# Attention values and denominators in one full-width matmul over [V|ones|V], shifted V and odd bias tables copied by DMA, and newly searched priorities

## The chip, the cores and the metric

The kernel runs as one program on the 8 cores of one Trainium2 chip. Cores 0 to 3 are one die, 4 to 7 the other. Cores 0 and 4 hold the beginning of a sequence and run one of two programs in the kernel ("first"); the other six run the second ("rest"). The metric is the time in microseconds (us) on the device of the slowest core. Some executions fall into a slower state, in which the cores of one die show a lower granted TensorE clock and the time is some per cent longer; only executions in the fast state are compared here. PE, DVE, ACT, POOL and SP are the engines (TensorE, VectorE, ScalarE, GpSimd, SyncE); on this kernel POOL issues the transfers of weights and SP those of outputs and small things.

## The reference

Four residual layers over one stream of 2 x 8192 tokens of width 1024, with 16 meta tokens put in front. Layers 0 and 3 mix by attention, layer 1 by a short gated convolution, layer 2 by pooling; a SwiGLU network follows each. The change touches the attention only:

```python
# 16 heads, 4 KV heads, head width 64, window 128, block 128
qkv = h @ w_qkv + b_qkv
...
s_band = einsum('bnqkgd,bnskd->bnkgqs', qb, k_band) + bias_band      # 2 blocks of keys
s_meta = einsum('bnqkgd,bmkd->bnkgqm', qb, km) + bias_meta           # 16 meta keys
p = softmax(concatenate([s_meta, s_band, sink_b], axis=-1))
o_r = einsum('bnkgqm,bmkd->bnqkgd', p_meta, vm) + einsum('bnkgqs,bnskd->bnqkgd', p_band, v_band)
return concatenate([o_m, o_r], axis=1) @ w_o + b_o
```

## The kernel before

The tokens of a core are worked in three groups, so there are 12 steps of a mixer and a network (layer 0 to 3 times group 0 to 2). The host program builds a list of operations with their dependences, and a list scheduler, steered by tables of priorities found by a search, puts them into one fixed order for each engine.

One unit of attention takes 64 queries of 4 heads for two KV heads: scores (PE, two row-tiled matmuls side by side), exponential (ACT), multiplication with a table of exponentials of the bias (DVE, into sb_P), values and denominators (PE), logarithm and exponential for the reciprocal of the denominator (ACT), product (DVE).

```python
# values: two KV heads side by side, 64 columns of the array each; then ones for the denominator
def av(e):
    for c, vf in ((0, va), (1, vb)):
        for kv in range(2):
            e.matmul(psum[kv*64:(kv+1)*64, O, 0:W], lhsT=vf(2*p+kv), rhs=P[...], start=(c==0), stop=(c==1))
    for c in range(2):
        for kv in range(2):
            ins = e.matmul(psum[kv*64:(kv+1)*64, O, 256:256+W], lhsT=one1, rhs=P[...], start=(c==0), stop=(c==1))
g.op("pe",  ..., av, R=[Pv, ...] + vk, W=[O], tag="av")
g.op("act", ..., R[:, 0:W] = Ln(bank(O)[:, 256:256+W]),  tag="den")
g.op("act", ..., R[:, 0:W] = Exp(-R[:, 0:W]),            tag="rden")
g.op("dve", ..., Q[:, ...] = bank(O)[:, 0:W] * R[:, 0:W], tag="omul")
...
# V of a block is kept three times: sb_Vt, and shifted with the meta tokens' V in sb_Vu and sb_Vw
g.op("act", ..., VU[0:64, sl, :] = VT_[0:64, sl, :],   tag="vu")
g.op("act", ..., VW[64:nr, sl, :] = VT_[64:nr, sl, :], tag="vw")
...
# the score of a unit lists the keys of V (vk) among what it reads, so it waits for V as well
g.op("pe", ..., sc, R=qk + kk + vk, W=[S], tag="score")
```

den and omul of one unit are one instruction each, of all 128 partitions: KV head 0 lies in partitions 0 to 63 and KV head 1 in 64 to 127 at the same columns.

The softmax here doesn't subtract the row's maximum and nothing guards it: scores larger than these inputs give would overflow.

## Time and profile before

| | before |
|---|---|
| time, median of 5 executions | 2690.76 us (2686.96 to 3039.39) |
| spans of the cores in the profiled execution | 2661.1 to 2669.8 us, clock 0.996 to 0.998 |
| PE, DVE, ACT busy on the slowest core (2) | 2628.2, 1565.4, 1331.8 us |
| PE idle on that core (span less busy) | 41.6 us |

The page of the profile gives, for the slowest core, busy time with its share of the span, and the chain of waits that ended last:

```profile
span 2669.8 us, 51871 instructions; the slowest of 8 cores (2661.1 to 2669.8 us)
...
PE 2628.2 (98%) x18296; PEld 1673.7 (63%) x18296; DVE 1565.4 (59%) x3259; ACT 1331.8 (50%) x2651; POOL 500.9 (19%) x951
...
PE 93%; DMA 2%; ACT 2%; issue 1%; DVE 1%; POOL 0%; POOLq 0%; DVEq 0%; ACTq 0%
...
```

The table of stretches gives the busy time of each engine in a stretch (start and end in us, length; then PE, weight loads, DVE, ACT, POOL, each with its count of instructions; clock, DMA share, GB/s):

```profile
...
core 2: us, PE busy (x) PEld busy (x) DVE busy (x) ACT busy (x) POOL busy (x), PEclk, DMA share, GB/s
0.00:140.00 140.00, 121.47 (x1033) 79.75 (x1034) 88.71 (x161) 97.47 (x189) 22.61 (x46) 0.95 0.58 126
140.00:440.00 300.00, 293.80 (x2253) 183.17 (x2252) 194.43 (x360) 194.43 (x399) 53.93 (x102) 1.00 0.67 106
440.00:1840.00 1400.00, 1396.17 (x9054) 880.20 (x9052) 822.43 (x1854) 603.56 (x1172) 275.92 (x522) 1.00 0.70 108
1840.00:2440.00 600.00, 597.24 (x4550) 395.59 (x4549) 349.19 (x670) 343.19 (x712) 114.67 (x217) 1.00 0.73 112
...
```

Of PE's 41.6 us of idle, 18.5 lie before 140 us, and 12.8 between 140 and 2440 us, although layers 0 and 3 with their attention lie in 20 to 440 and about 1700 to 2440 us. PE hardly ever waits, so only less work on PE, or an earlier start, can help. That is what the waits of PE on this core say too (what was waited for: us in all, times, longest):

```profile
...
PE ps L1464 <- DVE sb_P L1474: 6.8, 7, 3.6
PE ps L1216 <- ACT sb_sq L1210: 3.7, 3, 2.5
...
PE ps L1499 <- DVE sb_P L1474: 1.1, 1, 1.1
...
```

The groups of the instructions that the change splits (count after the x, busy us, then mean ns of one; then idle time before them), the product on DVE of core 2 first:

```profile
...
L1512 DVE TENSOR_TENSOR sb_qo<-ps,sb_R 128x256 bf16<-128x256 f32 x108 | 43.4, 416 | 10.0 <-ACT sb_R L1511 9.6 <-issue 0.3
...
```

and on ACT, the exponential (L1511) and the logarithm (L1510):

```profile
...
L1511 ACT ACTIVATE sb_R<-sb_R 128x256 f32<-128x256 f32 x128 | 51.0, 417 | 1.7 <-ACT sb_R L1510 0.4
L1510 ACT ACTIVATE sb_R<-ps 128x256 f32<-128x256 f32 x128 | 47.7, 381 | 57.5 <-PE ps L1505 54.0 <-DVE sb_h L1299 2.3 <-DVE sb_g L1852 0.2
...
```

### The profile page before, as it was taken

To read this page: it belongs to the slowest core of one execution; us is meant where nothing else is said; L and a number is where in the kernel's file an instruction comes from. 1 tells how busy PE (TensorE), PEld (TensorE's weight loads), DVE (VectorE), ACT (ScalarE), POOL (GpSimd) and SP (SyncE) were. 2 spreads that over 40 slices of the span, in tenths; PEclk is the share of its full clock that TensorE was granted. 3 is DMA by queue.
4 is the path that set the end of the run, shared out by engine and by line. 5 is a ranking of instruction groups with operands and counts; after the bars stand their busy time and mean duration, and the time that the engine had idled before them with its cause. 6 is when DMAs were issued, how large, how long until landed. Compare 5 with 4: busy or idle time off the path is not lost.

```text
span 2669.8 us, 51871 instructions; the slowest of 8 cores (2661.1 to 2669.8 us)
## 1 busy us (share of the span) xinstructions
PE 2628.2 (98%) x18296; PEld 1673.7 (63%) x18296; DVE 1565.4 (59%) x3259; ACT 1331.8 (50%) x2651; POOL 500.9 (19%) x951
## 2 busy tenths in 40 slices
PE   8999999999999999999999999999999999999998
PEld 5556665666666666655666666566566777656665
DVE  5785467455455555675685667446554665665534
ACT  6794566344243424353545534464553854744533
POOL 2021121211122212211111222112112221111110
PEclk9999999999999999999999999999999999999999
DMA  7476675766677767767657787658658878857873
GB/s 161 99 109 106 102 111 88 115 104 102 102 113 107 111 107 109 116 101 106 103 88 110 115 125 120 108 87 135 101 76 130 115 108 133 130 90 104 151 108 85
DMA packets 143446, 293.07 MB, mean 110 GB/s; under 512 B 15968, under 2 KB 22256, under 8 KB 142928
## 3 DMA queue, kind: packets, MB, share of 16 engines
q0 software_dynamic: 135840, 280.19, 67.6%
q1 hardware_dynamic: 7344, 9.47, 1.3%
q8 instruction: 154, 2.52, 0.4%
q14 instruction: 108, 0.88, 0.1%
HBM read 550.27 MB, written 8.28 MB: 209 GB/s over the span
## 4 chain that ended last, share of the span: by engine, by line
PE 93%; DMA 2%; ACT 2%; issue 1%; DVE 1%; POOL 0%; POOLq 0%; DVEq 0%; ACTq 0%
PE ps L1288 88%; PE ps L1499 1%; PE ps L1464 1%; PE ps L1505 1%; PE ps L1403 1%; PE ps L1806 1%; DMA sb_h<-x 0%; DMA sb_P<-xh 0%; DVE sb_P L1474 0%; DMA sb_ring<-ffn_gu 0%; DMA sb_ring<-attn_o 0%; DMA sb_ring<-attn_q 0%; PE ps L1228 0%; ACT sb_sq L1210 0%; ACT sb_ms L1139 0%
## 5 line engine op out<-in xcount | busy, mean ns | idle before, releaser
L1288 PE MATMUL ps<-sb_aF,sb_ring 128*128 128x384 bf16 (+4 forms) x8576 | 1342.5, 314 | 5.9 <-DVE sb_g L1852 1.6
L1288 PEld LDWEIGHTS ps<-sb_aF,sb_ring 128*128 128x128 bf16 x8576 | 826.3, 98 | 481.5 <-issue 39.0
L1288 PE MATMUL ps<-sb_g,sb_ring 128*128 128x384 bf16 (+4 forms) x4400 | 680.6, 315 | 2.9 <-DVE sb_g L1255 1.8
L1288 PEld LDWEIGHTS ps<-sb_g,sb_ring 128*128 128x128 bf16 x4400 | 427.8, 98 | 242.0 <-issue 11.8
L1848 DVE TENSOR_TENSOR sb_t<-sb_t,ps 128x384 f32<-128x384 f32 (+4 forms) x528 | 275.8, 523 | 431.5 <-ACT sb_t L1846 424.3
L1842 ACT ACTIVATE sb_t<-ps 128x384 f32<-128x384 f32 (+4 forms) x528 | 243.3, 461 | 497.0 <-PE ps L1288 494.5
L959 POOL DMA_DIRECT2D sb_ring<-ffn_gu x528 | 279.6, 534 | 1015.0 <-PE ps L1288 929.1
L1210 ACT ACTIVATE sb_sq<-sb_h 128x768 bf16<-128x768 f32 (+4 forms) x216 | 170.6, 796 | 427.2 <-DVE sb_h L1299 261.5
L1299 DVE TENSOR_TENSOR sb_h<-ps,sb_h 128x384 f32<-128x384 f32 (+4 forms) x432 | 226.8, 525 | 204.7 <-PE ps L1288 203.7
L1852 DVE TENSOR_TENSOR sb_g<-sb_t,ps 128x384 bf16<-128x384 f32 (+4 forms) x528 | 274.5, 522 | 108.7 <-PE ps L1288 100.6
L1844 ACT ACTIVATE sb_t<-sb_t,sb_ones 128x384 f32<-128x384 f32 (+4 forms) x528 | 310.3, 589 | 30.2 <-ACT sb_t L1842 0.7
L1288 PE MATMUL ps<-sb_aM,sb_ring 128*128 128x384 bf16 (+4 forms) x1952 | 322.6, 317 | 1.7 <-DMA sb_ring<-attn_q 0.9
L1846 ACT ACTIVATE sb_t<-sb_t 128x384 f32<-128x384 f32 (+4 forms) x528 | 261.8, 497 | 28.4 <-ACT sb_t L1844 0.7
L1288 PEld LDWEIGHTS ps<-sb_aM,sb_ring 128*128 128x128 bf16 x1952 | 189.9, 98 | 109.7 <-issue 7.7
L959 POOL DMA_DIRECT2D sb_ring<-ffn_dn x192 | 101.7, 532 | 592.5 <-PE ps L1288 519.3
L1474 DVE TENSOR_TENSOR sb_P<-ps,sb_ms 128x1024 bf16<-128x1024 f32 x128 | 154.7, 1220 | 64.2 <-ACT ps L1469 63.9
L1288 PE MATMUL ps<-sb_qo,sb_ring 128*128 128x384 bf16 (+3 forms) x1024 | 163.3, 315 | 1.4 <-DMA sb_ring<-attn_o 1.4
L1469 ACT ACTIVATE ps<-ps 128x1024 f32<-128x1024 f32 (+2 forms) x134 | 130.4, 990 | 10.6 <-PE ps L1464 10.1
L1288 PEld LDWEIGHTS ps<-sb_qo,sb_ring 128*128 128x128 bf16 x1024 | 99.8, 98 | 55.8 <-issue 2.8
L1301 DVE SCALAR_TENSOR_TENSOR sb_h<-ps,sb_cst,sb_h 128x384 f32<-128x384 f32 (+4 forms) x144 | 82.4, 583 | 65.7 <-PE ps L1288 51.8
L1223 DVE TENSOR_TENSOR sb_sq<-sb_sq 128x768 bf16<-128x768 bf16 (+4 forms) x156 | 81.7, 526 | 47.9 <-ACT sb_sq L1210 46.7
L1255 DVE SCALAR_TENSOR_TENSOR sb_aF<-sb_h,sb_cst,sb_rs 128x384 bf16<-128x384 f32 (+4 forms) x192 | 103.8, 581 | 3.6 <-ACT sb_rs L1233 2.9
(119 smaller groups left out, 1384.3 us busy)
## 6 DMA issues: line engine op xcount, KB each, us to landing
sb_ring<-ffn_gu POOLq DMA_DIRECT2D x528, 256.0 KB, 6.2
sb_ring<-ffn_dn POOLq DMA_DIRECT2D x192, 352.0 KB, 5.9
sb_ring<-conv_in POOLq DMA_DIRECT2D x72, 256.0 KB, 5.7
sb_ring<-attn_o POOLq DMA_DIRECT2D x48, 256.0 KB, 9.9
sb_ring<-attn_q POOLq DMA_DIRECT2D x40, 256.0 KB, 7.0
sb_ring<-conv_out POOLq DMA_DIRECT2D x24, 256.0 KB, 6.8
sb_ring<-attn_k POOLq DMA_DIRECT2D x11, 512.0 KB, 7.4
sb_ring<-attn_v POOLq DMA_DIRECT2D x11, 512.0 KB, 12.9
```

The source lines that it names most:

```text
L959: e.dma_start(out=ring[:, o.off:o.off + o.n], in_=o.src).then_inc(sem(o.dop[0]), 16)
L1210: lambda e, sv=sv, c=c: e.activation(out=ap(sv)[:, 0:2 * n].rearrange("p (a b) -> p a b", a=2), in_=src(2 * c, 2 * c + 2), func=AF.Square),
L1255: lambda e, k=k: e.scalar_tensor_tensor(out=dst[:, k, c0 - goff:c1 - goff], in0=h1(k, c0, c1), scalar=gam[:, gi * KC + k:gi * KC + k + 1], ...
L1288: i = e.matmul(bank(pv)[:, 0:n], lhsT=wap(u, woff + k * wst, M), rhs=rhs(k), start=(k == 0), stop=(k == nk - 1))
L1299: f = lambda e: e.tensor_tensor(out=h1(m, c0, c1), in0=bank(pv)[:, 0:n], in1=h1(m, c0, c1), op=ALU.add)
L1469: g.op("act", act_ns(4 * W), lambda e: e.activation(out=sp3(), in_=sp3(), func=AF.Exp, scale=0.125), R=[S], W=[S], tag="exp")
L1474: g.op("dve", dve_ns(4 * W), lambda e: e.tensor_tensor(out=pp(), in0=sp3(), in1=ebt, op=ALU.mult), R=[S, ("eb", p, odd)], W=[Pv], tag="ebm ...
L1842: g.op("act", act_ns(n), lambda e, pg=pg, tv=tv, n=n: e.activation(out=ap(tv)[:, 0:n], in_=bank(pg)[:, 0:n], func=AF.Exp, scale=-1.0), R=[ ...
L1844: g.op("act", act_ns(n, True, True), lambda e, tv=tv, n=n: e.activation(out=ap(tv)[:, 0:n], in_=ap(tv)[:, 0:n], func=AF.Ln, bias=ones1[:], ...
L1846: g.op("act", act_ns(n, True), lambda e, tv=tv, n=n: e.activation(out=ap(tv)[:, 0:n], in_=ap(tv)[:, 0:n], func=AF.Exp, scale=-1.0), R=[tv] ...
L1848: g.op("dve", dve_ns(n), lambda e, pg=pg, tv=tv, n=n: e.tensor_tensor(out=ap(tv)[:, 0:n], in0=ap(tv)[:, 0:n], in1=bank(pg)[:, 0:n], op=ALU ...
L1852: g.op("dve", dve_ns(n), lambda e, pu=pu, tv=tv, n=n, fj=fj, a=a, b=b: e.tensor_tensor(out=gg[:, fj, a - goff:b - goff], in0=ap(tv)[:, 0:n ...
```

## The change

The intent: PE is the limit, and every change between row-tiled scores, column-tiled values and full-width projections costs PE a gap. If values and denominators come from one full-width matmul, they need no mode of their own. A stored block of V becomes [V0|ones|V1] for each pair of KV heads, 192 columns. Columns 0 to 127 give V0 over its denominators, columns 64 to 191 the denominators over V1. ACT, which den now burdens more, is relieved of the V copies and of the copies that make the odd bias tables; these become transfers issued by SP. The tables of priorities were searched anew. Only the attention of the first group of layer 0 stays tiled.

```diff
-MODES = {"score": 1, "scorem": 1, "av": 2, "avm": 2, "vmeta": 2}
+MODES = {"score": 1, "scorem": 1, "av": 2, "avm": 2}
+TILED_AV = ((0, 0),)
+VB = 384
-RING = 16400
+RING = 15744
...                                                   # PLACES: all priorities and places of loads are new
-                    g.op("act", ..., act(lambda o_=o_: o_, lambda i_=i_: i_, AF.Copy), ..., tag="ebodd")
+                    g.op("sp", ..., lambda e, o_=o_, i_=i_: e.dma_start(out=o_, in_=i_), ..., dma="odd%d" % nload[0], tag="ebodd")
...
-            g.op("act", act_ns(256, True), lambda e: e.copy(out=VU[0:64, sl, :], in_=VT_[0:64, sl, :]), ..., tag="vu")
-            g.op("act", act_ns(256, True), lambda e: e.copy(out=VW[64:nr, sl, :], in_=VT_[64:nr, sl, :]), ..., tag="vw")
+            v_copy(VU, slice(0, 64), sl, "Vu")       # e.dma_start on SP
+            if 2 * t + 3 <= lay.blocks[5][-1]:
+                v_copy(VW, slice(64, nr), sl, "Vw")
...                                                   # V of the meta tokens projected once, not twice
+                def av(e):
+                    for kv in range(2):
+                        for c in cs:
+                            o_ = p * 192 + kv * 64
+                            ins = e.matmul(bank(O)[:, 256 * kv:256 * kv + W], lhsT=vs[c][:, o_:o_ + 128], rhs=pr(kv, c), start=(c == cs[0]), stop=(c == cs[-1]))
+                g.op("pe", 2 * len(cs) * pe_ns(W), av, R=[Pv] + vk, W=[O], tag="avf" + m_)
+                for kv in range(2):
+                    g.op("act", act_ns(W), ... ap(R)[kv*64:(kv+1)*64, 0:W] = Ln(bank(O)[64-kv*64:128-kv*64, 256*kv:256*kv+W]), tag="den")
...
+            for rows, o_ in ((slice(0, 128), 0),) if tiled else ((slice(0, 64), 0), (slice(64, 128), 256)):
+                g.op("dve", dve_ns(W), ... Q[rows, ...] = bank(O)[rows, o_:o_+W] * ap(R)[rows, 0:W], tag="omul")
```

The two KV heads now stand at different columns of the bank, so den and omul become two instructions of 64 partitions each.

## The prediction

> **What bounds it now.** TensorE. The page of the slowest core (core 2, one of six with the "rest" program) gives a span of 2669.8 us, PE busy 98%, DVE 59%, ACT 50%; the chain of waits is 93% PE. The table of stretches leaves PE idle about 24 us up to 140 us, 13 us in the next 2500 us, 10 us in the last 30 us. After the start only less PE time can help.
>
> **What the change does to PE.** Streaming time stays. In PE's timeline two 64-column value matmuls of width 256 run at once, a pair every 0.11 us, so a unit of 8 takes 0.44 us; four full 128-column matmuls of width 256 also start every 0.11 us. What goes is the change of array mode. The Trainium skill, "TensorEngine Tiling (Array Packing)", Key Properties, says that changing the tiling mode drains the engine. The trace agrees: the last pair before a full matmul takes 0.21 us instead of 0.11; 8 full 384-wide matmuls take 1.40 us instead of 1.31 when a tiled group follows. A switch costs 0.10 to 0.11 us. Counted in the instruction orders, switches fall from 347 to 236 (rest program) and 355 to 252 (first program): 10 to 12 us. The meta tokens' V is projected once, not twice: 16 matmuls of 0.11 us, 1.8 us. The first program skips the empty block, under 1 us. Sum: about 13 us, nearly all on the chain.
>
> **What it adds and moves.** Outside the first group, logarithms and products are split in halves: 112 more on ACT (0.38 us each, +42 us) and 112 more on DVE (0.41 us, +46 us). ACT loses 70 V copies of 0.40 us (28 us) and 12 table copies (estimate 7 to 9 us). Net ACT +6 us, DVE +46 us, in attention stretches where DVE is 50 to 80% busy, so little should reach PE. The first group, where DVE and ACT are 75 to 90% busy and PE waits for them, stays tiled and only gets the relief.
>
> The V copies become some 70 small transfers that need a few us to land (existing transfers of that queue: 2.4 to 20 us). Score, exponential and bias multiply lie in between; I expect a few short waits, mostly early. About 1 MB of table copies comes where the DMA share is already 0.85 to 1.05.
>
> **Priorities.** The new order was searched with a slower DMA at the start. In before, a late chunk of x kept PE waiting 3.6 us near 84 us, with a half-rate clock for about 2 us after. Filler matmuls between 20 and 130 us fall from 76 to 45 and 45 to 31, but the initial ones rise from 110 to 169 and 52 to 123. Net gain 2 to 5 us in the first 130 us.
>
> **Prediction.** 2689.6 - 13 - 4 = 2672 us, 8 in 10 between 2656 and 2686. Faster by over 2%: 0.03; within 2%: 0.95; slower: 0.02.
>
> **What would show it.** Value matmuls of 128 columns, 448 in the rest program, every 0.11 us, no gap around them. PE idle in 140 to 2640 us stays at 10 to 18 us; V copies seldom among what PE waits for. DVE busy rises to about 1610 us.
>
> **What would make it wrong.** A switch hides under other work (half the gain). V transfers stuck behind weight traffic stall value matmuls (5 to 15 us lost). The DVE halves delay h additions that PE needs. Weight loads of 128 columns don't hide under 256-wide matmuls (up to 5 us). Or the new order removes nearly all early idle (10 us more).

## The result, and the profile after

| | before | after |
|---|---|---|
| time, median of 5 executions | 2690.76 us (2686.96 to 3039.39) | 2729.02 us (2726.25 to 2964.77) |
| ratio of the fast runs | | 1.014, 95% interval 1.012 to 1.016 |
| spans in the profiled execution, cores 0 to 3 | 2661.1 to 2669.8 | 2692.9 to 2704.1 |
| the same, cores 4 to 7 | 2662.2 to 2668.2 | 2706.5 to 2725.0 |
| mean clock of dies 0 and 1 | 0.998, 0.997 | 0.992 to 0.995, 0.983 to 0.987 |

A ratio is the mean time of one kernel's fast runs over that of the other's fast runs of the same rounds, so it is not quite the ratio of the medians. The kernel became 1.4% slower, outside the predicted range. (Before's own executions on this chip took 2687 to 2691 us, though the longest span in its profile is 2669.8 us and before took 2670 to 2672 us on the four chips used later; the record has no spans of these executions, so what held them up stays open.) On this chip the second die ran the changed kernel at a lower clock in all executions. Since no other chip showed this (see the control run), I read the changes on core 2 of the undisturbed die, 2669.8 to 2695.8 us, and on core 0 for the first program, 2663.4 to 2696.8 us.

The page of the slowest core (7) after:

```profile
span 2725.0 us, 51500 instructions; the slowest of 8 cores (2692.9 to 2725.0 us)
...
PE 2648.9 (97%) x17860; PEld 1684.6 (62%) x17860; DVE 1619.9 (59%) x3378; ACT 1348.0 (49%) x2681; POOL 501.1 (18%) x951
...
PE 87%; ACT 4%; DVE 3%; DMA 3%; issue 3%; SPq 1%; POOL 0%; DVEq 0%; ACTq 0%; POOLq 0%
...
```

The stretches of core 2 after:

```profile
...
0.00:140.00 140.00, 113.83 (x1025) 77.85 (x1026) 88.73 (x162) 88.00 (x168) 21.10 (x43) 0.96 0.55 133
140.00:440.00 300.00, 293.11 (x2062) 185.64 (x2059) 205.21 (x387) 200.71 (x408) 57.82 (x109) 1.00 0.70 114
440.00:1840.00 1400.00, 1394.19 (x9103) 878.70 (x9104) 846.51 (x1892) 623.64 (x1226) 270.90 (x511) 1.00 0.69 108
1840.00:2440.00 600.00, 574.46 (x4104) 381.27 (x4102) 354.84 (x701) 328.70 (x674) 113.03 (x214) 0.99 0.67 108
...
```

PE lost 7.6 us of work before 140 us and 22.8 us between 1840 and 2440 us, in the attention of layer 3. Between 140 and 2640 us PE stood idle for 38.3 us, against 12.9 before and the 10 to 18 us that the prediction named as its sign. DVE and ACT rose only a little: DVE was busy 1617.7 us on this core, up 52.

What PE waits for after, on core 2:

```profile
...
PE ps L1495 <- DMA sb_Vu<-sb_Vt: 20.8, 3, 16.0
PE ps L1495 <- DVE sb_P L1506: 7.7, 15, 0.9
...
PE ps L1302 <- DVE sb_t L1868: 5.1, 10, 1.0
PE ps L1302 <- DVE sb_g L1872: 3.2, 9, 0.9
...
PE ps L1547 <- DVE sb_P L1506: 2.8, 6, 0.7
...
```

and on core 0, of the first program:

```profile
...
PE ps L1230 <- ACT sb_sq L1224: 24.8, 3, 17.9
PE ps L1495 <- DMA sb_Vu<-sb_Vt: 13.2, 7, 3.2
PE ps L1537 <- DVE sb_P L1517: 6.6, 1, 6.6
...
```

New are the waits of the score (line 1495) for the copied table sb_Vu, 20.8 us in three waits, one of 16.0, and a scatter of short waits for DVE. The timeline shows the long one (start, duration, engine; in brackets the idle time before and what ended it):

```profile
...
2271.51 3.43 SPq L1898 DMA_DIRECT2D out<-sb_h  x2
...
2275.03 3.91 SPq L1419 DMA_DIRECT2D sb_Vu<-sb_Vt  x1
...
2292.09 0.40 PE L1495 MATMUL ps<-sb_qo,sb_Kn 64*128 64x256 bf16 x2 [16.05 <-DMA sb_Vu<-sb_Vt]
...
2292.64 2.74 PE L1302 MATMUL ps<-sb_aF,sb_ring 128*128 128x384 bf16 x8
...
2295.85 1.64 PE L1302 MATMUL ps<-sb_aF,sb_ring 128*128 128x384 bf16 x8
...
```

and the summary of transfers from 2255 to 2295 us on this core (KB each, median us from issue to landing):

```profile
...
out<-sb_h SPq DMA_DIRECT2D x16, 128.0 KB, 19.3
...
sb_Vu<-sb_Vt SPq DMA_DIRECT2D x3, 48.0 KB, 11.6
...
```

Sixteen output stores of 128 KB of the first group (two of them are the first line above) stand ahead of the V copies on SP, issued from 2255.4 us on, and take a median of 19.3 us to land. The copy of 48 KB issued at 2275.03 us lands behind them, and a score stands still for 16.05 us. (The score does not use V; it waits because the program lists V among its reads. No run took that dependence away.) The eight projections right after it run at about half speed, 2.74 us against 1.64 for the next eight, the first of which are still slow.

The split instructions after: half the partitions take as long as all (420 against 416 ns, 378 against 381 ns), so 108 omul became 216 and their busy time doubled, on DVE of core 2:

```profile
...
L1555 DVE TENSOR_TENSOR sb_qo<-ps,sb_R 64x256 bf16<-64x256 f32 x216 | 89.4, 420 | 21.7 <-ACT sb_R L1553 14.0 <-DVE sb_qo L1555 0.5
...
```

and the logarithm on ACT after:

```profile
...
L1551 ACT ACTIVATE sb_R<-ps 64x256 f32<-64x256 f32 x216 | 80.4, 378 | 25.8 <-PE ps L1547 17.7 <-DVE sb_qo L1555 1.5
...
```

### The profile page after: what moved, and what is told of

Same layout as the page of the kernel before. It is cut to its first block, busy times and chain, and to the rows that moved or that the text cites. A ratio compares the mean times of both kernels' runs of the same rounds, so it can differ in the third digit from the quotient of the medians.

```text
span 2725.0 us, 51500 instructions; the slowest of 8 cores (2692.9 to 2725.0 us)
## 1 busy us (share of the span) xinstructions
PE 2648.9 (97%) x17860; PEld 1684.6 (62%) x17860; DVE 1619.9 (59%) x3378; ACT 1348.0 (49%) x2681; POOL 501.1 (18%) x951
## 4 chain that ended last, share of the span: by engine, by line
PE 87%; ACT 4%; DVE 3%; DMA 3%; issue 3%; SPq 1%; POOL 0%; DVEq 0%; ACTq 0%; POOLq 0%
PE ps L1302 82%; PE ps L1547 1%; PE ps L1495 1%; PE ps L1429 1%; ACT ps L1500 1%; DMA sb_Vu<-sb_Vt 1%; DVE sb_P L1506 1%; DMA sb_ms<-sb_ms 1%; ACT sb_R L1551 1%; ACT sb_t L1864 1%; PE ps L1826 1%; ACT sb_t L1866 1%; DMA sb_cst<-cst 1%; SPq L1898 0%; DVE sb_qo L1555 0%
## 5 line engine op out<-in xcount | busy, mean ns | idle before, releaser
L1302 PE MATMUL ps<-sb_aF,sb_ring 128*128 128x384 bf16 (+4 forms) x8576 | 1369.1, 317 | 14.6 <-DVE sb_t L1868 6.3
L1555 DVE TENSOR_TENSOR sb_qo<-ps,sb_R 64x256 bf16<-64x256 f32 x224 | 91.9, 416 | 22.5 <-ACT sb_R L1553 14.4
```

The costliest lines, as they stand in the source:

```text
L1302: i = e.matmul(bank(pv)[:, 0:n], lhsT=wap(u, woff + k * wst, M), rhs=rhs(k), start=(k == 0), stop=(k == nk - 1))
```

## The experiments

Theories at the start: QUEUE (V copies queue behind output stores), COPY (V copies by DMA are late anyhow), START (loads of x come later), SWITCH (the full-width matmul is worth its 10 to 12 us and something else eats it) and, as a rival that came up on the way, HALVES (den and omul in halves cost PE more than the switches did). They ran later, on four chips on which the kernel before took 2670 to 2672 us.

To compare groups of cores I use the mean span of cores 0 and 4 ("first") and of the other six ("rest"), from the profiled fast execution:

| run | time | ratio to before (fast executions) | first | rest |
|---|---|---|---|---|
| before (first chip's profile) | | 1 | 2665.4 | 2665.2 |
| after_again, the changed kernel | 2707.72 | 1.0136 | 2700.0 | 2697.5 |
| f1 stores behind | 2698.87 | 1.0112 | 2696.0 | 2681.9 |
| f2 common start | 2709.6 | 1.0149 | 2698.2 | 2698.4 |
| f3 both | 2697.34 | 1.0101 | 2694.6 | 2683.3 |
| f4 both, tiled values | 2705.82 | 1.0135 | 2703.2 | 2685.1 |
| f5 start, copies on ACT | 2690.75 to 2697.3 | 1.0076 | 2688.4 | 2687.2 |
| f6 as f5, tiled and unsplit | 2682.61, 2684.34 | (unclear) | 2680.9 | 2676.5 |
| f6_again | 2681.9 to 2701.92 | 1.0073 | 2679.8 | 2676.0 |
| f7 as f6, odd tables on ACT | 2697.39 | 1.0101 | 2679.0 | 2690.4 |
| b1 before, full-width on rest | 2722.32 | 1.0191 | 2665.6 | 2716.7 |
| b4 before, halves on rest | 2721.81 | 1.0189 | 2664.4 | 2715.9 |
| b5 before, omul halves on rest | 2699.2 | 1.0103 | 2662.9 | 2691.4 |
| b2 before, V copies by DMA | 2677.22, 2678.27 | (unclear) | 2675.2 | 2667.4 |

(A single time is the median of all executions, slow ones too; of the fast ones alone it is 2705.98 for after_again, 2708.2 for f2, 2722.27 for b1, 2721.37 for b4, 2696.56 for b5 and 2697.21 for f7. Where slow ones were many, the fast ones are listed. "Unclear" means that too few fast executions were left for an interval. In the rounds of these runs before's means lie between 2662 and 2666 us, first and rest.)

### First attempts, which let the scheduler move: e1, e2, e3, e4

Run e1 takes the nine issues that stand ahead of the program branch on POOL away from the kernel before; in the changed kernel they had gone, since the new places of the loads differ between the two programs.

```diff
-PRE = {"pe": 0, "act": 0, "dve": 4, "pool": 9, "sp": 0}
+PRE = {"pe": 0, "act": 0, "dve": 4, "pool": 0, "sp": 0}
```

> The kernel before, with its 9 common DMA issues of POOL (those made ahead of the branch between the two programs) put behind the branch; the changed kernel has 0 of them. Theory START (the changed kernel starts late because no load is issued ahead of the branch): first x load issued at about 3 us (rest cores) and 11 us (first cores) instead of 1.6 us; first projection 1 to 2 us later on rest cores, about 10 us later on first cores; slowest core 5 to 10 us longer than before. Rival ORDER (the searched order and the extra DVE and ACT work cost the time, not the start): within 3 us of before.

Measured: 2674.33 us, ratio 1.0014 (0.9991 to 1.0037). Cores 0 and 4 rose to 2670.8 and 2671.7 us, about 6 us above their profile before; the rest stayed. A later start costs the first program something and the slowest core almost nothing.

Run e2 gives the changed kernel equal places for the first loads in both programs, by its tables:

```diff
-               "ld2": "Q0", "ld3": "Q0", "ld4": "V", "ld5": "Q0", ... "ld8": "Q1"      # first
-               "hX": "Q1", "ld1": "V", "ld2": "K", "ld3": "V", "ld4": "K", "ld5": "Q0" # rest
+               "ld2": "K", "ld3": "K", "ld4": "K", "ld5": "K", ... "ld8": "Q2"
+               "hX": "Q2", "ld1": "K", "ld2": "K", "ld3": "K", "ld4": "K", "ld5": "K"
```

> The changed kernel with the positions of the first x loads and of the constants put back so that 9 issues of POOL are again common to both programs and stand ahead of the branch. START: first projection at about 20 us on all cores (it was at 26.5 on core 2 and 37.3 on core 0); rest cores 5 to 8 us shorter than the changed kernel, first cores 13 to 18 us; time down by 5 to 10 us, since rest cores were the slowest. ORDER: within 3 us of the changed kernel.

Measured: 2729.06 us, ratio 1.0213 (1.0183 to 1.0242), a miss. The scheduler had made another order, with new waits: on core 2 24.1 us for sb_Vu, 8.9 us in one wait for sb_P, 6.4 us for weights. The run says nothing of the start, but it says that another order can cost about 20 us (1.0213 against 1.0136 for the changed kernel in its control run).

Run e3 was to hang the first group's output stores behind the V copies by a dependence:

```diff
-                g.op("sp", ..., e.dma_start(out=out_d[k, ...], in_=h1(k, a, b)), R=[("h", k, t)], dma="out", tag="store")
+                late.append(... the same operation, made later with after=copies of V of the attention that follows ...)
```

> The changed kernel with the output stores of groups 0 and 1 of the last layer issued only after all V copies of the next group's attention (same queue, same copies, same sizes). Theory QUEUE (V copies wait behind 16 output stores in the SP queue, and the scores wait for them): the 16 us wait of PE near 2275 us on rest cores goes (under 2 us left), and with it the half-rate clock after it; rest cores 15 to 18 us shorter than the changed kernel, first cores 8 to 12 us. Rival LATENCY (each V copy is slow by itself, because of weight traffic): the wait stays over 8 us, time within 4 us of the changed kernel. ORDER: within 4 us too.

Measured: 2716.51 us, ratio 1.017 (1.0147 to 1.0193). The edit missed its aim. It hung the stores on the copies of the second group's attention, but they are issued during the third's, so the 16 stores still stood ahead and a score still waited 16.8 us. It tests nothing.

Run e4 was to have the full-width matmuls alone, with before's priorities and all copies on ACT:

```diff
-    "first": { ... new tables ... }, "rest": { ... }      DMA_FIRST = (60000.0, 300.0)
+    "first": { ... before's tables ... }, "rest": { ... } DMA_FIRST = (0.0, 330.0)
-            g.op("sp", ..., e.dma_start(out=T[rows, sl, :], in_=VT_[rows, sl, :]), ...)     # and the odd tables
+            g.op("act", ..., e.copy(out=T[rows, sl, :], in_=VT_[rows, sl, :]), ...)
```

> The full-width value matmuls, the single projection of the meta V and the split logarithms and products alone: V copies and odd bias tables stay on ACT, priorities and DMA figures of the scheduler are those of before. Theory SWITCH (110 fewer array mode switches of 0.10 to 0.11 us and 16 fewer matmuls are worth 11 to 14 us, and the extra halves on ACT and DVE do not reach PE): 8 to 14 us faster than before, PE waits in 140 to 2640 us grow by less than 5 us. ORDER: at least as slow as before, since DVE has 46 us and ACT 42 us more to do.

Measured: 2776.58 us, ratio 1.0397 (1.0373 to 1.042), the opposite of what SWITCH expects. PE on core 2 waited 30.8 us in 39 waits for sb_P. I first blamed the order, since it too had been made anew. The runs below show that this was only part of it.

From here on the finished order is kept. Each edit acts after the scheduler has run, or changes only what an operation does at its place, and a comparison of the traces shows the order of work of the engines that it does not touch unchanged.

### The changed kernel, untouched: after_again

> The changed kernel itself, not edited, as the base for the runs that undo one part of it. If the run whose edit missed its aim (2716.5 us, ratio 1.017) was in effect a repeat of it: 2712 to 2720 us, ratio 1.015 to 1.018, both dies at the same clock, and the wait of 16 us for sb_Vu on the cores of the second program. If the 2729 us of the first timing belong to the kernel and not to that chip's second die: 2725 or more.

Measured: 2707.72 us (fast executions 2705.93 to 2707.72), ratio 1.0136 (1.0114 to 1.0158), both dies alike. This is the base for the runs f1 to f7, which ran earlier and on other chips, so I compare ratios. With both dies alike the changed kernel is still 35 us slower than before, so the loss does not rest on the low clock of the first chip's second die. (That the ratio is the 1.014 of the first chip is partly chance: there both kernels took about 20 us more than here.) It also shows that e3, at 1.017, was a little slower than what it was taken for; whether its stores or its chip did that is open.

### QUEUE and START: f1, f2, f3

```diff
         sched, t = schedule(g, make_pools, PLACES["first" if FIRST else "rest"])
+        sp = sched.seq["sp"]                                                             # f1, f3
+        last = max(i for i, o in enumerate(sp) if o.tag in ("vu", "vw"))
+        early = [o for o in sp[:last] if o.tag == "store"]
+        sched.seq["sp"] = [o for o in sp[:last + 1] if o.tag != "store"] + early + sp[last + 1:]
+        for i in range(5): byname["ld%d" % (i + 1)].start = 530.0 * i                    # f2, f3
+        for i in range(4): sched.uload[i] = (u, deps, 530.0 * (5 + i))                   # K, V, Q0, Q1
```

> The changed kernel with its order of work frozen: only on SP, the 16 output stores of the first group (all stores that stood ahead of a V copy) are taken out of the finished order and put behind the last V copy. PE, DVE, ACT and POOL keep their order to the instruction. QUEUE theory (V copies queue behind the stores): the score's wait for sb_Vu near 2276 us, 12.8 to 16.8 us on the six cores of the second program in the runs so far, falls below 4 us, and these cores' spans fall by 10 to 17 us; the first program's two cores, which had no such long wait, by 0 to 5. Against about 2716 us for the changed kernel on this chip (ratio 1.017), about 2703 us, ratio 1.010 to 1.013. Rival (V copies by DMA are slow in any case, behind weights as much as behind stores, or the time only comes back as a later wait): a wait of 8 us or more stays near there, ratio 1.015 to 1.018.

> The changed kernel with its order frozen, except that the first nine POOL issues of both programs are put into one common order (four loads of x, constants, K, V, Q0, Q1), so that all nine stand ahead of the branch as in the kernel before. PE, DVE, ACT, SP keep their order. START theory: the first load of x is issued at about 1.6 us on every core again (was 11.1 and 3.1), the first projection starts at about 20 us (was 37 on cores 0 and 4, 26.5 on the rest); spans of cores 0 and 4 fall by 10 to 17 us, of the rest by 4 to 7; slowest core about 2710 us, ratio 1.013 to 1.016. Rival (the start is slack: the DMA stream of weights or the vector engine paces the first 140 us, as the run that removed the common issues from the kernel before suggested): spans of the rest fall by less than 2 us, ratio 1.016 to 1.018, and the time comes back as waits between 40 and 140 us.

> Both edits of order at once (stores behind the last V copy, nine common issues ahead of the branch), everything else frozen. If QUEUE and START hold and add up: spans of the six cores of the second program fall by 15 to 23 us against the changed kernel, to about 2690 to 2700, ratio about 1.007 to 1.010; what is left over the kernel before is then in the order of the work (waits on the vector engine at 60 to 140 us and small waits in the attention steps). If they don't add up, because a wait taken away only uncovers another: 1.012 or more.

f1: ratio 1.0112 (1.0094 to 1.013). The rest cores fell by 15.6 us in the mean, the first by 4. QUEUE holds. The waits of core 2:

```profile
...
PE ps L1495 <- DVE sb_P L1506: 7.9, 14, 1.8
...
PE ps L1495 <- DMA sb_Vu<-sb_Vt: 4.3, 1, 4.3
...
```

The 16 us are gone and no such wait came back. The time of the chip fell by less, 7 us between the medians of the fast executions, because cores 0 and 4 set it now.

f2: ratio 1.0149 (1.0128 to 1.0171), no gain, so START falls in the sense that matters. The start itself did come back, as the timeline of core 0 shows:

```profile
...
22.95 1.51 PE L1302 MATMUL ps<-sb_g,sb_ring 128*128 128x400 bf16 x8 [1.33 <-DVE sb_g L1269]
...
32.66 2.83 PE L1302 MATMUL ps<-sb_g,sb_ring 128*128 128x400 bf16 x8 [6.46 <-ACT sb_KX L1371]
...
```

The first projection ran at 22.95 us where the changed kernel has it at 37.3 us. The second then waited 6.46 us for ACT, a value matmul near 64 us 8.4 us for sb_P behind an odd table on its way by DMA, and cores 0 and 4 ended 1.8 us earlier than in the control. The second line also shows the half-rate clock after a wait: 2.83 us for eight matmuls that took 1.51. (The Trainium skill, "TensorE: Matmul & The Clock Gate", What's actually happening, has the clock halved after an idle window of about 3.4 us; this wait was 6.46 us, the one in the changed kernel 16.05, and the trace agrees in both. But on core 0 of f2 the granted clock also stood at 0.50 after waits of 2.74 us, near 391 us, and 2.03 us, near 2544 us, so a shorter wait is not safe.)

f3: ratio 1.0101 (1.0083 to 1.0119). Its rest cores are where f1's are. START adds nothing there, and 1 us on the first.

### SWITCH, looked at in the new order: f4

```diff
-                            ins = e.matmul(bank(O)[:, 256 * kv:256 * kv + W], lhsT=vs[c][:, o_:o_ + 128], rhs=pr(kv, c), ...)
+                            ins = e.matmul(psum[kv * 64:(kv + 1) * 64, O.slot[0], 256 * on:256 * on + W], lhsT=one1[:, :] if on else vs[c][:, o_:o_ + 64],
+                                           rhs=pr(kv, c), ...)       # half-height den and omul kept
```

> As the run with both edits, but the full-width value matmuls are put back to pairs of column-tiled ones, with their own ones matmuls for the denominator, at the same places in the same order; the half-height den and omul instructions, the DMA copies and all else stay. The count of mode changes on PE rises from 236 to 386 (second program) and from 252 to 414 (first). SWITCH theory at the 0.10 to 0.11 us read from the trace of before: 14 to 17 us slower than the run with both edits, ratio to it 1.005 to 1.007. Rival (the change of mode is hidden or costs PE nothing where it waits for exp anyway): less than 5 us.

Measured: ratio 1.0135 against f3's 1.0101, 8.5 us in the medians. The first cores lost 8.6 us, the rest 1.8. So with the halves kept, full-width matmuls do help here: the first cores by about half of what their 162 switches cost, the rest by little. On core 2 PE's busy time rose by 13.9 us (2621.6 to 2635.5, that is 0.093 us for each of 150 switches; 13.1 us in the mean of the six rest cores, 16.2 of the first two), but the span by 3.0 and idle fell by 10.9. In this order PE has idle time into which a switch can go unseen. It is the first sign that PE no longer sets the pace in attention.

### The full-width matmul alone, in before's own order: b1, and its rivals b4 and b5

Here the kernel before keeps its order on every engine, and the six rest cores get the new layout of V and the new matmuls in place (to make room, some small tables were laid over others; weights stay, and the copies of V stay on ACT, half again as wide).

```diff
 def av(e):
+    if wide:                                  # rest program, all but the first group of layer 0
+        for kv in range(2):
+            for c in range(2):
+                ins = e.matmul(bank(O)[:, 256 * kv:256 * kv + W], lhsT=[V|ones] or [ones|V] of 128 columns, rhs=P[...], ...)
+        return ins
```

> The kernel before with its own finished order of work kept to the instruction on every engine; only on the six cores of the second program the value and ones matmuls of all attention units outside the first group of the first layer become four full-width matmuls over [V|ones|V] at the same place, and den and omul become two half-height instructions at the same place. V copies stay on ACT, the ring of weights keeps its size, no priorities change. Mode changes on PE fall from 347 to 235 on these cores. SWITCH theory at 0.10 to 0.11 us each: spans of these six cores fall by 9 to 12 us (from 2660 to 2670 to about 2650 to 2660); cores 0 and 4 stay where they are and then set the time, ratio 0.995 to 0.999. Rival (the switch was hidden, or the half-height den and omul cost as much as is won): spans of the six cores within 4 us of before.

Measured: 2722.32 us, ratio 1.0191 (1.0171 to 1.0212). The rest cores became about 51 us slower instead of 9 to 12 faster; cores 0 and 4, which had not been changed, stayed. Nothing else was moved, so neither copies by DMA nor priorities can be the cause. b4 leaves the tiled matmuls of before and only splits den and omul:

```diff
-return e.activation(out=R[:, 0:W], in_=bank(O)[:, 256:256 + W], func=AF.Ln)
+for r in (slice(0, 64), slice(64, 128)):
+    ins = e.activation(out=R[r, 0:W], in_=bank(O)[r, 256:256 + W], func=AF.Ln)
...                                                # omul likewise; in b5 omul only
```

> The kernel before in its own order; only den and omul are split into two half-height instructions each, on the six cores of the second program and outside the first group of the first layer, as in the run with full-width matmuls. The value matmuls stay pairs of column-tiled ones. HALVES theory (112 more DVE instructions of 0.42 us and 112 more ACT instructions of 0.38 us at the place where the next score or projection waits): spans of these six cores rise by 35 to 60 us, most of the 50 us of the full-width run, ratio 1.012 to 1.022. Rival (the full-width matmuls themselves delay: four matmuls into one bank, values and denominators ready only at the last): spans rise by less than 12 us.

> As the run with both halves, but only omul is split (DVE +46 us); den stays one instruction on ACT. If DVE is what PE waits for in attention: at least half of the loss of the run with both halves stays, spans of the six cores up by 20 to 40 us. If the halves on ACT lead the chain: under 10 us. If each costs its own share, about half.

Measured: b4 2721.81 us, ratio 1.0189 (1.0164 to 1.0213), the same as b1. b5 2699.2 us, ratio 1.0103 (1.0078 to 1.0127), about half. HALVES holds, and each half has its part: omul on DVE 26 us, den on ACT another 25 (means of the rest cores). The waits of PE on core 2 of b4:

```profile
...
PE ps L1464 <- DVE sb_P L1474: 16.5, 23, 3.4
PE ps L1499 <- DVE sb_qo L1523: 7.5, 16, 1.0
PE ps L1499 <- DVE sb_P L1474: 6.2, 11, 1.6
...
PE ps L1288 <- DVE sb_t L1859: 4.6, 8, 1.2
...
```

and of b5:

```profile
...
PE ps L1464 <- DVE sb_P L1474: 10.6, 19, 1.5
PE ps L1499 <- DVE sb_qo L1517: 4.3, 12, 0.8
...
```

In before, the score (L1464) waited 6.8 us in 7 waits for sb_P; with halves 16.5 us in 23, and values (L1499) wait 7.5 us for earlier products of omul. The sums of busy time over all stretches of core 2, in b4:

```profile
...
sum 2760.00, PE 2638.13 PEld 1672.36 DVE 1620.54 ACT 1387.52 POOL 500.89; mean PE 527.63 PEld 334.47 DVE 324.11 ACT 277.50 POOL 100.18
```

and in b1:

```profile
...
sum 2760.00, PE 2626.72 PEld 1669.71 DVE 1621.63 ACT 1391.95 POOL 500.85; mean PE 525.34 PEld 333.94 DVE 324.33 ACT 278.39 POOL 100.17
```

The two differ in the value matmuls, with 347 mode changes against 235, and in the layout of V, whose wider copies cost ACT 4.4 us. On this core PE's busy time is 2638.13 against 2626.72 us, 11.4 us less, or 0.102 us for each switch. But that it fits so well is luck: on the other five rest cores the difference is 1.7 to 6.6 us, 6.1 in the mean of all six (`prof b4_before_halves --core all --windows 0:2800`, and the same of b1). PE's busy time also changes with its waits: b4 has before's PE instructions, all in the same order, and is busy 9.8 us longer in that mean. The span of core 2 is 2720.6 against 2719.1 us. What b1 gains in busy time is lost as idle time (81.1 to 88.0 us in the mean of the six):

| core 2 | span | PE busy | PE idle | DVE busy |
|---|---|---|---|---|
| before | 2669.8 | 2628.2 | 41.6 | 1565.4 |
| b5, omul in halves | 2688.5 | 2629.8 | 58.7 | 1618.3 |
| b4, den and omul in halves | 2720.6 | 2638.1 | 82.5 | 1620.5 |
| b1, the same and full-width | 2719.1 | 2626.7 | 92.4 | 1621.6 |

### COPY: b2 and f5

b2 is the kernel before with the V copies moved from ACT to transfers on SP, at the places of the same start:

```diff
+        for o in [o for o in act if o.tag in ("vu", "vw") and o.key_]:
+            o.eng, o.dma = "sp", "v" + o.key_
+            sp.insert(i, o)                                  # i: by start
-lambda e: e.copy(out=VU[0:64, sl, :], in_=VT_[0:64, sl, :])
+lambda e: e.dma_start(out=VU[0:64, sl, :], in_=VT_[0:64, sl, :])
```

> The kernel before with its order kept; only the copies of V to the shifted tables leave ACT and are issued as transfers on SP, at the places where their start in the schedule falls (tiled matmuls, ACT odd tables and everything else stay). COPY theory (a transfer costs latency and queues behind weights and stores where an ACT copy took 0.40 us): PE waits for the shifted V tables of 8 to 25 us in sum on every core, spans up by as much, ratio 1.004 to 1.010. Rival (the copies by DMA harm only through the searched order that came with them): waits below 4 us, ratio 0.999 to 1.002.

Measured: two fast executions of 2677.22 and 2678.27 us, and three slow ones, so no interval; against 2670.18 us for before in the same rounds that is 7 to 8 us. The first cores rose by 10 us with 8.9 us of waits for sb_Vu in two waits, the rest by 2 although core 2 also waited 8.9 us in two. The waits were where COPY had them, the loss was at the low end and came mostly on cores 0 and 4.

f5 is the changed kernel with the common start and the V copies put into ACT's order:

```diff
+        moved = [o for o in sp if o.tag in ("vu", "vw")]
+        for o in moved:
+            o.eng, o.dma = "act", None
+            act.insert(i, o)                                 # the first place after V is ready
-lambda e: e.dma_start(out=T[rows, sl, :], in_=VT_[rows, sl, :])
+lambda e: e.copy(out=T[rows, sl, :], in_=VT_[rows, sl, :])
```

> The changed kernel with its order frozen and the nine common issues ahead of the branch, and with the V copies as ACT copies put into the order of ACT where V is ready; stores and all else stay. COPY theory: no wait for a shifted V table is left; against the run with both edits of order (2697 us, ratio 1.010) cores 0 and 4 fall by 8 to 13 us (they waited 11.6 us in four waits at 140 to 440 us), the other six by 2 to 6; about 2684 us, ratio 1.004 to 1.007. Rival (the waits only move to exp or to the vector engine): ratio 1.009 or more.

Measured: ratio 1.0076 (1.0056 to 1.0097). The first cores fell by 6.2 us against f3, less than expected, and the rest rose by 3.9 where I had them fall. ACT is burdened by the halves already; core 2's wait of 5 us for sb_Vu went, but its idle time rose from 58.1 to 63.5 us. On the rest cores the copies by DMA were no bad bargain once no store stood ahead of them (f5 put its copies into ACT's frozen order where V is ready, without a new search).

### The new order with before's instructions: f6, f6_again, f7

f6 is f5 with tiled values, and den and omul in one piece: the first of each pair does the whole, the second is taken out.

```diff
+        gone = {o.id: o.twin for o in g.ops if o.tag in ("den", "omul") and o.twin is not None}
+        sched.seq[e] = [o for o in sched.seq[e] if o.id not in gone]          # and in all dependences
```

> As the run with the copies on ACT, but with pairs of column-tiled value matmuls and whole-height den and omul again: nearly the instructions of before, in the order of after. ORDER theory (the rest of the loss is the searched order itself): the time stays 15 us or more above before, ratio 1.006 to 1.010, and the full-width matmuls then are worth 5 to 12 us (the run with tiled matmuls put back lost 8 us to its twin, half-height den and omul kept). Rival (the rest of the loss is the half-height den and omul on DVE and ACT): this run is as fast as or faster than its full-width twin, ratio below 1.004.

> The run of before's instructions in the order of after once more, unchanged, since only one of its executions was in the fast state (2682.6 us). Expected 2680 to 2685 us, ratio 1.003 to 1.006, so 5 to 14 us faster than its full-width twin (2690.8 us at best, ratio 1.0076).

Measured: f6's two fast executions are 2682.61 and 2684.34 us, against 2690.75 to 2697.3 for f5 on the same chip in the same rounds. f6_again had 2681.9, 2682.9 and 2684.29, and one of 2701.92 that counts as fast, hence a ratio of 1.0073 with a wide interval (1.0024 to 1.0123). The mean spans fell by 7.5 us on the first cores and 10.7 on the rest against f5. So in the order that was searched for it the full-width matmul with its halves is a net loss of about 8 to 10 us. Neither expectation of f6 was met whole: it beat its twin, as the rival had it, but stayed 12 to 14 us above before, nearer to ORDER. On core 2 the pair reads: f5 busy 2621.6, idle 63.5; f6 busy 2631.0, idle 42.8.

f7 puts the odd bias tables back on ACT as well:

```diff
+        moved = [o for o in sp if o.tag in ("ebodd",)]        # into ACT's order, as the V copies
```

> As f6_again, and the odd bias tables are copied by ACT instead of by DMA, in the order of ACT where their source is ready. On core 0 the wait of a value matmul for sb_P (8.2 us at about 70 us, behind the transfer of an odd table) falls below 2 us and cores 0 and 4 fall by 4 to 8 us, to 2673 to 2677; the six others change by less than 3 us. Slowest core 2675 to 2683, ratio 1.002 to 1.005. Rival (the start of cores 0 and 4 is paced by the chain of norm and projections, so the time comes back as another wait before 140 us): less than 2 us on cores 0 and 4.

Measured: ratio 1.0101 (1.0076 to 1.0125), a miss. On core 0 the wait of 8.2 us for sb_P went, others came (3.5 and 1.8 us for ACT), and cores 0 and 4 gained 1 us: the rival was right. The rest became 14 us slower, which neither theory had; core 3 shows one new wait of 6.0 us for sb_t (its 5.6 us of waits for weights stood at 5.7 in f6). In this order the odd tables are better made by DMA; the run put the copies into ACT's frozen order without a new search, so it does not show what they cost at searched places.

No run beat the kernel before, which stays the fastest.

## Why the prediction was wrong

- **"2689.6 - 13 - 4 = 2672 us".** Both terms were to be gains. The first exists on PE, but in before's order it came back as idle time (b4 to b1), and in the new order it reached the first cores (8.6 us, f3 to f4) and hardly the rest (1.8); the second was a loss, and two terms that stood in the text as "little" and "a few short waits" were the large ones.
- **"A switch costs 0.10 to 0.11 us ... 10 to 12 us".** The size was about right. From f3 to f4, 150 more switches added 13.1 us of PE's busy time in the mean of the six rest cores, 0.087 us each, and 162 more added 16.2 us on the first two, 0.100 us each. The 0.102 us of core 2 from b4 to b1 is no proof, since the mean of six cores there is 6.1 us. The Trainium skill's "TensorEngine Tiling (Array Packing)", Key Properties, says that a change of tiling mode drains the engine; 0.09 to 0.10 us is what that drain comes to here.
- **"Net ACT +6 us, DVE +46 us, in attention stretches where DVE is 50 to 80% busy, so little should reach PE".** This is the step that failed. The busy times were right (DVE 1617.7 us on core 2, about 1610 predicted), and so was the cost of an instruction: half height is no cheaper. The Trainium skill, "VectorE: DVE Perf Modes", Why tensor_reduce can't reduce along partition axis, says that the engine streams along the free dimension with an independent pipeline for each partition, and 420 against 416 ns agrees. But more than half of it reached PE. In before's order, 112 omul and 112 den more made the rest cores 51 us slower, 0.45 us for each unit out of 0.80 us of added work. In the order searched for it the toll was smaller: taking the halves and the full-width matmuls back (f5 to f6) cut idle time by 20 us in the mean of the rest cores, though PE had 9.5 us more to do. (b4 is harder on ACT than the change: it keeps the V copies there, so ACT is busy 56 us more than before on core 2, in the changed kernel 15.) DVE's share of 65% between 140 and 440 us in before says that DVE has free time, not that it has it when a unit needs it. The waits say where: scores stand for sb_P and values for the product of an earlier unit. My reading is that the units follow each other through few buffers, so that added instructions lengthen a chain from score to product that had just fitted; the runs show the waits and their sum, not the buffer that closes the chain.
- **"I expect a few short waits, mostly early".** Wrong. Core 2 waited 20.8 us for sb_Vu, 16.0 of it in layer 3. I had named the danger ("stuck behind weight traffic", 5 to 15 us) but looked at the wrong neighbour: the stores shared SP's own queue. The Trainium skill, "DMA: Bandwidth & Descriptors", Queues, rings and completion order, says that SP owns one row of rings, one on each of the 16 DMA engines, that each of these takes descriptors in ring order, and that the semaphore's increment lands after every earlier write of that DMA engine. f1 agrees: with the stores behind the copies and nothing else moved, the rest cores fell by 15.6 us. I had not looked in the finished order for what stands ahead of the copies.
- **"Net gain 2 to 5 us in the first 130 us".** Wrong. PE's work before 140 us fell from 121.5 to 113.8 us on core 2 and from 112.8 to 99.9 on core 0. I counted filler matmuls and did not see that the nine common issues ahead of the branch had gone. Yet f2 gave them back without a gain: the new order waits elsewhere before 140 us.

The staircase from after to before, as far as it was taken apart, in ratios: 1.0136; 1.0112 with the stores behind; 1.0101 with the common start too; 1.0076 with the copies on ACT instead; about 1.005 with tiled values and unsplit den and omul (f6's fast executions over before's median of the same rounds). The runs stood on different chips and the intervals are about 0.002 wide to each side, so the small steps are rough. In spans the rest cores of after_again are 32.3 us above before, all of it idle time (40.1 to 72.4 us in the mean; PE's busy time stayed at 2625 us, where 13 us less had been forecast): f1 takes back 15.6 us, f1 to f5 gives up 5.3, f5 to f6 takes back 10.7, and 11.3 remain. The last 0.5%, 13 us, belongs to what f6 keeps: the new order, the odd tables by DMA, one projection of the meta V, the wider copies of V and the smaller ring of weights (RING 15744 instead of 16400). f7 speaks against the odd tables. I take the order for the cause of most of it, but no run shows that, nor which part of it; the smaller ring was not tested. Since the scheduler answers every edit with another order, the question can't be asked by undoing one priority.

## What to carry to other kernels

Before trading PE time for more instructions on another engine, ask what a single unit of work must pass through on its way back to PE, and try the added instructions alone in the old order; the engine's average share does not answer it. A small transfer on a queue takes the place of whatever stands ahead of it there, so read the finished order of that queue before taking a copy off a compute engine. When a scheduler reorders everything, freeze its result and edit that, or the experiment measures the scheduler.

## What the Trainium skill lacked or had wrong

- "TensorEngine Tiling (Array Packing)" says that a change of mode drains the engine but gives no price: here PE's busy time rose by 0.087 us a change (150 changes, 13.1 us, mean of six cores) and by 0.100 us (162 changes, 16.2 us, mean of two), f3 to f4.
- No page says in so many words that an instruction on 64 partitions costs as much as one on 128: DVE 420 against 416 ns, ACT 378 against 381 ns for 256 columns. For DVE it follows from "VectorE: DVE Perf Modes"; "ScalarE: Activation LUTs" would be the place for ACT.
- The tiling page doesn't warn that stacking [V|ones|V] puts the two heads at different columns and so doubles the instructions that read the bank: in before's order 51 us were lost (b4) for 6.1 us of PE's busy time won (b4 to b1, mean of six cores).
- "DMA: Bandwidth & Descriptors", Anatomy of one DMA, fits 2.0 us plus bytes over 436 GB/s for a transfer issued by GpSimd, an estimate of 2.1 us for 48 KB. On SP's queue such a copy took 11.6 us in the median behind stores of 128 KB that took 19.3 us each. The page has the order of a queue, not what waiting in it costs.
- "TensorE: Matmul & The Clock Gate", What's actually happening, gives an idle window of about 3.4 us before the clock halves. In f2 a granted clock of 0.50 followed waits of 2.74 and 2.03 us on core 0 too, so a wait need not be that long.
